# Two-layer encoder trunk: FFN's first weights split in the mixer's dead tiles, eps squares on other queues, a bank of its own for one edge product, weights in order of use

## Chip, cores and metric

The kernel runs on one core of a Trainium2 chip. The metric is the device time of one execution in microseconds; a kernel's time is the median of several executions. Between two kernels, a difference of some 0.2% is about what such a measurement can tell from none.

## What is computed

The trunk has two layers. Each is a mixer with RMS norms before and after it and a residual, then a squared-ReLU MLP (FFN) with the same frame. The two requests have 512 and 256 tokens, and the width is 1024. Cut to what matters here:

```python
for i in range(DEPTH):
    h = rms_norm(x, norm_mix_pre[i])
    mix = even_mixer(h, ...) if i % 2 == 0 else odd_mixer(h, ...)
    x = x + rms_norm(mix, norm_mix_post[i])
    h = rms_norm(x, norm_ffn_pre[i])
    f = jnp.square(jax.nn.relu(h @ ffn_w1[i])) @ ffn_w2[i]      # 1024 -> 4096 -> 1024
    x = x + rms_norm(f, norm_ffn_post[i])
```

## The kernel before, in words

All tiles hold features on the 128 partitions and tokens along the free dimension, 768 tokens in all (the 512 of the first request, the 256 of the second). A product in full precision is made of three matmuls per 128-row step: weights and activations are each split into a high and a low part (`hi` by a copy on ScalarE, `lo` by a subtraction on VectorE), and the three products hi*hi, lo*hi and hi*lo accumulate in one PSUM bank. The accumulators `acc` of the residual stay in SBUF.

**Order of work.** A scheduler with priorities lays out one program in order per engine; within an engine nothing overtakes. `tick`, `defer` and `settle` of `Trunk` put small finishing steps some number of matmul groups later than the step that they follow. `weave` mixes a list of fill steps into a list of main steps at a given rate.

**From mixer to FFN.** The mixer ends with `quarter`s of its output projection. The last one finishes the residual in three blocks of 256 tokens: `PostNorm` squares (`sq`, L451), sums the squares over partitions on TensorE (L272), makes `rstd` (L281 to L286), and writes the new `acc` (L481, L485) and the normalised `h` (L360, L361). FFN's class `Strassen` then multiplies by the first weight matrix in 32 units of 128 columns. The first four units go block by block (`units_a`), with weights split by `Strassen.first` (L540, L541) into tiles of the FFN's own pool, called `ht`. While four more units run, `blocks` builds the sums of activation blocks that a Strassen scheme (7 products instead of 8 on 2x2 blocks) needs (L573 to L580, tiles `tb`, `tt`, `ht`). From there `pair` computes two units at a time from weight sums `sw` (L606 to L610). The first and the last such pair (u = 3 and u = 15) are edge pairs: `X`, a PSUM tile, takes a first product "11", ScalarE copies it away (`p1`, written as `sg`, L660), and then a second product "12" by "21" is added into the same tile before it is put away (`put`).

**FFN's second matrix.** Class `Strassen2` (the functions `weights`, `add`, `keep`, `prep`) runs over pairs of hidden groups; j = 0 to 3 counts the output quarters within a pair. `weights` splits the sums and the raw weights (L794, L795) in the order s1 and s2 (`s12`), "12" and "22" (`raw`), s3 and s4 (`s34`), "11"; L854 adds a product from PSUM to `acc`. After the Strassen groups come plain quarters 4 to 7. With the group (2,3) runs a fill, `eps_sums`: it reloads the layer's input (`ex`), squares it on ScalarE (L404), adds the eight squares on GpSimd (L406) and sums them over partitions on TensorE (L414). Only the following post-norm needs the result.

**Odd mixer's start.** `sums` makes a block's `rstd` as a row (`rb`), and `by_token` turns `rb` into a column per token with TensorE (L426) and copies it on VectorE (L428).

Of the kernel before, what the change touches and what calls it, by code (L numbers as in the profile page):

```python
# [45 lines left out]
class Trunk:  # L46
# [292 lines left out]
class PreNorm:  # L339
# [55 lines left out]
    def eps_sums(self, xD, part):  # L395
# [12 lines left out]
        yield  # L408
        yield
        for s in range(2):  # L410
            ps = T.tps()
            n = SEQN[s] // CH
            for j in range(n):
                nc.tensor.matmul(ps[:, j:j + 1], lhsT=tot[s][:, j * CH:(j + 1) * CH], rhs=T.ones[:, 0:1], start=True,  # L414
                                 stop=True)
            v = T.cp.tile([128, 8], F32, tag="rsq_a", name="rsq_a", bufs=2)[:, 0:n]
            nc.vector.tensor_scalar(out=v, in0=ps[:, 0:n], scalar1=1.0 / 1024, scalar2=EPS, op0=ALU.mult, op1=ALU.add)
            nc.vector.scalar_tensor_tensor(out=self.rc[s][:, 0:n], in0=v, scalar=1024 * EPS, in1=v, op0=ALU.mult, op1=ALU.mult)
        yield

    def by_token(self, b):
        s, c0, n = b
        T, nc = self.T, self.T.nc
        ps = T.tps()
        for j in range(n // CH):
            nc.tensor.matmul(ps[:, j:j + 1], lhsT=self.rb[s][:, c0 + j * CH:c0 + (j + 1) * CH], rhs=T.ident[:, 0:1],  # L426
                             start=True, stop=True)
        nc.vector.tensor_copy(self.rc[s][:, c0 // CH:(c0 + n) // CH], ps[:, 0:n // CH])  # L428
        self.done.add(b)

# [89 lines left out]


class Strassen:

# [119 lines left out]
    def pair(self, u, edge):  # L643
# [19 lines left out]
        X = T.dps()[:, 0:HF]  # L663
        self.product(w["11"], "11", X, True, False)
        p1 = copy(X)
# [22 lines left out]
        else:  # L688
# [27 lines left out]
class StrassenK:  # L716
# [58 lines left out]

    def weights(self, j, first):

# [12 lines left out]
        def parts(n):  # L790
            return [T.wp.tile([128, 1024], F32R, tag=t, name=t, bufs=4)[:, 0:n] for t in ("whi", "wlo")]

        def split(x, hi, lo):
            nc.scalar.activation(out=hi, in_=x, func=AF.Copy)  # L794
# [8 lines left out]
        tt = (nc.vector if first else nc.gpsimd).tensor_tensor  # L803
        tt(out=s1, in0=a21, in1=a22, op=ALU.add)
# [4 lines left out]
        pl = parts(1024)  # L809
        split(raw[1], *pl)  # L810
        for m, name in enumerate(("12", "22")):
            w[name] = [t.rearrange("p (k m c) -> p m k c", k=4, m=2)[:, m] for t in pl]
# [28 lines left out]
    def group(self, gs, last):  # L841
# [5 lines left out]
        for j in range(4):  # L847
            w = self.weights(j, j == 0)
            u2 = self.u2[j]

            def add(ps, m, half):
                with hp():
                    for a, c in self.blocks(2 * j + m, half):
                        nc.vector.tensor_tensor(out=a, in0=a, in1=ps[:, c], op=ALU.add)  # L854

# [62 lines left out]

def ffn(T, layer, pre, xsrc, nxt, xdst):
    tc, nc = T.tc, T.nc  # L920
    with tc.tile_pool(name=f"ffn{layer}", bufs=1) as pool:
        hidD = tc.dram_tile([8, 4, 128, NT], F32, name=f"hidD{layer}")
        S = Strassen(T, pool, pre, pre.xs, layer, hidD)

        def evac(s, o, c0, n, m):
            gt = T.g0 if n == 512 else T.g1
            r = gt("fr")
            with tc.high_priority():
                nc.scalar.activation(out=r, in_=o, func=AF.Relu)
                nc.scalar.activation(out=r, in_=r, func=AF.Square)  # L930
            nc.sync.dma_start(out=hidD[m // 4, m % 4][:, SEQ0[s] + c0:SEQ0[s] + c0 + n], in_=r)

        srcs = [S.src[m] for m in range(NSTD)]
        evacs = [partial(evac, m=m) for m in range(NSTD)]
        run(T.units_a(S.first(4), pre, evacs))
        T.settle()
        fill = S.blocks()
        for m in range(4, NSTD):
            weave(T.unit_a(srcs[m], pre.h, evacs[m], True), fill, 0.5)
        run(fill)  # L940
# [6 lines left out]
        for i, g in enumerate(GROUPS):  # L947
# [12 lines left out]
            if not end and isinstance(GROUPS[i + 1], tuple):  # L960
                fill = K.prep(GROUPS[i + 1])
            elif g == EQ:
                fill, per = pre.eps_sums(xsrc, K.part), 0.4
            weave(steps, fill, per)
# [597 lines left out]
def even_layer(T):  # L1562
    tc, nc, I = T.tc, T.nc, T.I
    with tc.tile_pool(name="p0", bufs=7) as pool:
# [75 lines left out]
        run(T.quarter(I["evO"][3], mix_load(T, E.mixD, 3, place=place), acc, False, pn))  # L1640
    return pn.pre
PPB = 4
# [236 lines left out]
def odd_layer(T, pre):  # L1879
    tc, nc, I = T.tc, T.nc, T.I  # L1880
    with tc.tile_pool(name="p1", bufs=7) as pool:
# [37 lines left out]
    return pn.pre  # L1919


def trunk(tc, I, y):
    with ExitStack() as ctx:
        T = Trunk(ctx, tc, I, y)
        T.setup()
        pre = even_layer(T)
        pre = ffn(T, 0, pre, T.xa, (0, 1), T.xb)
        pre = odd_layer(T, pre)
        ffn(T, 1, pre, T.xc, None, y)

# [92 lines left out]
```

## Time and profile before

| | us |
|---|---|
| median of 3 runs (2297.16 to 2301.91) | 2301.15 |
| the profiled execution's own time | 2302.54 |
| its span (first to last instruction) | 2300.8 |
| TensorE busy | 2204.1 (96%) |
| VectorE busy | 1672.8 (73%) |
| ScalarE busy | 1061.9 (46%) |
| GpSimd busy | 667.9 (29%) |

The span is what the profiler records between first and last instruction; the time lies 1.7 us above it. TensorE is the engine to read by: what it is not busy is 96.7 us, and beside that there are stretches where its clock is granted at half.

### The profile page before, as it was taken

The numbers are of one execution on the slowest core, as the hardware profiler recorded it, in microseconds if no ns is written. First come the engines' busy times: TensorE is split into PE (matmuls) and PEld (weight loads), VectorE is DVE, ScalarE is ACT, GpSimd is POOL, SyncE is SP. The second block draws the span as 40 slices with busy tenths as digits, with TensorE's granted clock in tenths as the row PEclk, the third lists the DMA queues.
The fourth block names the chain that finished last, engine by engine and source line by source line (L and its number), as shares of the span: only waits on it lengthen the run. The fifth ranks groups of instructions, "written<-read, shape, count | busy, mean of one in ns | idle before, by whom it ended". The sixth has DMA issues, their size and how long they took to land.

```text
span 2300.8 us, 39195 instructions
## 1 busy us (share of the span) xinstructions
PE 2204.1 (96%) x14360; PEld 2038.9 (89%) x14360; DVE 1672.8 (73%) x3491; ACT 1061.9 (46%) x2140; POOL 667.9 (29%) x666
## 2 busy tenths in 40 slices
PE   8999999999998999999899899999998999999897
PEld 7888888998888999999889888988888999999887
DVE  8969858756556866678567758788766866688566
ACT  6655454334334544444324415555644644454332
POOL 2335133311104244220704330111004244320714
PEclk9999999999999999999999999999999999999999
DMA  4445235446343333544344245444533344544342
GB/s 148 125 130 159 84 117 158 140 142 189 119 129 117 114 120 128 185 142 151 104 151 127 98 145 161 153 156 143 175 111 124 100 135 129 162 165 138 116 129 92
DMA packets 188896, 311.23 MB, mean 135 GB/s; under 512 B 18912, under 2 KB 119328, under 8 KB 188704
## 3 DMA queue, kind: packets, MB, share of 16 engines
q1 hardware_dynamic: 188704, 308.73, 42.5%
q8 instruction: 113, 1.85, 0.3%
q14 instruction: 79, 0.65, 0.1%
HBM read 234.64 MB, written 74.02 MB: 134 GB/s over the span
## 4 chain that ended last, share of the span: by engine, by line
PE 70%; DVE 18%; issue 4%; ACT 3%; DMA 3%; POOL 2%; SPq 0%; POOLq 0%; ACTq 0%; DVEq 0%
PE dps L208 6%; PE dps L209 6%; PE dps L210 6%; PE dps L154 4%; PE dps L152 4%; PE dps L153 4%; PE dps L187 3%; PE dps L627 3%; PE dps L628 3%; PE dps L629 3%; PE dps L189 3%; PE dps L188 3%; DVE acc L481 2%; PE mps L629 2%; PE mps L627 2%
## 5 line engine op out<-in xcount | busy, mean ns | idle before, releaser
L208 PE MATMUL dps<-mh,whi 128*128 128x256 f32 (+1 forms) x800 | 270.5, 338 | 1.2 <-DVE acc L219 1.1
L209 PE MATMUL dps<-mh,whi 128*128 128x256 f32 (+1 forms) x800 | 265.5, 332 | 0.0
L210 PE MATMUL dps<-mh,wlo 128*128 128x256 f32 (+1 forms) x800 | 264.8, 331 | 0.0
L187 PE MATMUL dps<-whi,h 128*128 128x256 f32 x864 | 260.4, 301 | 1.9 <-ACT gv L1695 1.5
L152 PE MATMUL dps<-h,whi 128*128 128x256 f32 (+1 forms) x728 | 251.7, 346 | 0.0
L189 PE MATMUL dps<-whi,h 128*128 128x256 f32 x864 | 245.7, 284 | 2.2 <-DVE h L361 2.2
L188 PE MATMUL dps<-wlo,h 128*128 128x256 f32 x864 | 245.4, 284 | 0.0
L154 PE MATMUL dps<-h,wlo 128*128 128x256 f32 (+1 forms) x728 | 243.1, 334 | 0.0
L153 PE MATMUL dps<-h,whi 128*128 128x256 f32 (+1 forms) x728 | 242.8, 334 | 0.0
L119 ACT ACTIVATE whi<-raw 128x1024 fp32r<-128x1024 f32 x140 | 147.7, 1057 | 162.6 <-PE dps L209 59.0
L120 DVE TENSOR_TENSOR wlo<-raw,whi 128x1024 fp32r<-128x1024 f32 x140 | 177.5, 1271 | 48.4 <-ACT whi L119 47.2
L187 PEld LDWEIGHTS dps<-whi,h 128*128 128x128 f32 x864 | 166.0, 192 | 13.7 <-issue 9.0
L188 PEld LDWEIGHTS dps<-wlo,h 128*128 128x128 f32 x864 | 166.4, 193 | 3.3 <-issue 2.2
L189 PEld LDWEIGHTS dps<-whi,h 128*128 128x128 f32 x864 | 166.0, 192 | 2.8 <-DVE h L361 2.8
L208 PEld LDWEIGHTS dps<-mh,whi 128*128 128x128 f32 x800 | 152.5, 191 | 17.4 <-DVE acc L219 2.6
L219 DVE TENSOR_TENSOR acc<-acc,dps 128x512 f32<-128x512 f32 (+1 forms) x208 | 100.7, 486 | 91.0 <-PE dps L210 90.9
L210 PEld LDWEIGHTS dps<-mh,wlo 128*128 128x128 f32 x800 | 152.1, 190 | 14.8
L455 POOL TENSOR_TENSOR sq<-sq 128x256 f32<-128x256 f32 x79 | 64.6, 818 | 345.0 <-ACT sq L451 344.6
L209 PEld LDWEIGHTS dps<-mh,whi 128*128 128x128 f32 x800 | 152.5, 191 | 13.5
L152 PEld LDWEIGHTS dps<-h,whi 128*128 128x128 f32 x728 | 138.6, 190 | 17.0 <-issue 4.9
L153 PEld LDWEIGHTS dps<-h,whi 128*128 128x128 f32 x728 | 138.8, 191 | 13.7 <-issue 1.7
L154 PEld LDWEIGHTS dps<-h,wlo 128*128 128x128 f32 x728 | 138.6, 190 | 13.5
(377 smaller groups left out, 6391.8 us busy)
## 6 DMA issues: line engine op xcount, KB each, us to landing
raw<-in_f SPq DMA_DIRECT2D x128, 512.0 KB, 3.9
hidD<-hc SPq DMA_DIRECT2D x104, 192.0 KB, 1.9
xt<-hidD SPq DMA_DIRECT2D x40, 384.0 KB, 3.8
rr<-acsD SPq DMA_DIRECT2D x48, 256.0 KB, 3.7
raw<-in_evB SPq DMA_DIRECT2D x24, 512.0 KB, 3.7
rl<-retD SPq DMA_DIRECT2D x48, 256.0 KB, 2.8
raw<-hidD SPq DMA_DIRECT2D x24, 512.0 KB, 3.8
stk<-qkD SPq DMA_DIRECT2D x96, 128.0 KB, 2.8
```

The lines of the kernel that those rows point to most:

```text
L119: nc.scalar.activation(out=hi, in_=raw, func=AF.Copy)
L120: nc.vector.tensor_tensor(out=lo, in0=raw, in1=hi, op=ALU.subtract)
L152: nc.tensor.matmul(o, lhsT=hi[:, k, :], rhs=hh[k][:, sl], start=k == 0, stop=False)
L153: nc.tensor.matmul(o, lhsT=hi[:, k, :], rhs=hl[k][:, sl], start=False, stop=False)
L154: nc.tensor.matmul(o, lhsT=lo[:, k, :], rhs=hh[k][:, sl], start=False, stop=k == NKT - 1)
L187: nc.tensor.matmul(o, lhsT=hh[k][:, sl], rhs=hi[:, k % 4, :], start=k == 0, stop=False)
L188: nc.tensor.matmul(o, lhsT=hh[k][:, sl], rhs=lo[:, k % 4, :], start=False, stop=False)
L189: nc.tensor.matmul(o, lhsT=hl[k][:, sl], rhs=hi[:, k % 4, :], start=False, stop=k == NKT - 1)
L208: nc.tensor.matmul(o, lhsT=hi[:, k, ms], rhs=hh[k][:, sl], start=k == 0, stop=False)
L209: nc.tensor.matmul(o, lhsT=hi[:, k, ms], rhs=hl[k][:, sl], start=False, stop=False)
L210: nc.tensor.matmul(o, lhsT=lo[:, k, ms], rhs=hh[k][:, sl], start=False, stop=k == 3)
L627: nc.tensor.matmul(o, lhsT=hi[:, k, :], rhs=hh[k], start=first and k == 0, stop=False, **f)
```

## The change

- `ffn_first` runs the first four units inside the mixer's pool, before it closes. Their weights are split in halves of 512 columns (L555 and L556 after) into 16 tiles called `fw`, which take the places of mixer tiles that nothing reads any more (`xtok`, `cr0`, `bc0`, `hb` in the even layer; `st0`, `ang`, `v` in the odd).
- `eps_sums` squares in place in one 128x768 tile per step, its adds go from GpSimd to VectorE, and `issue_after` puts both behind the last split and the last add of the Strassen groups on their own queues (order only, no semaphore).
- In an edge pair the product "12" by "21" gets a PSUM tile of its own, `V`, and VectorE adds `V` and `p1` into an SBUF tile (`c11`), four times in the kernel.
- For j = 3 `weights` splits in the order "11", `raw`, `s34`, `s12`.
- A block counts as done when its `rb` is written, `defer` keeps its list sorted, and the odd layer's `by_token` is deferred by 3 steps instead of 6.

```diff
     def defer(self, n, f):
         self.late.append([n, f])
+        self.late.sort(key=lambda i: i[0])
...
-        while b not in self.done:
+        while b not in self.done and self.T.late:
             self.T.late.pop(0)[1]()
...
-        T.defer(FT2, partial(self.by_token, b))
+        self.done.add(b)
+        T.defer(FT2 if self.first else FT3, partial(self.by_token, b))
...
-        tot = [T.g0("et"), T.g1("et")]
+        tot = part("et")
         for k in range(NKT):
-            x = part("ex")
+            x = part("ex") if k else tot
             nc.sync.dma_start(out=x, in_=xD[k])
-            for s in range(2):
-                xs = x[:, SEQ0[s]:SEQ0[s] + SEQN[s]]
-                nc.scalar.activation(out=xs if k else tot[s], in_=xs, func=AF.Square)
+            with ExitStack() as ctx:
+                for i in tail:
+                    ctx.enter_context(T.tc.issue_after(i.ins))
+                nc.scalar.activation(out=x, in_=x, func=AF.Square)
                 if k:
-                    nc.gpsimd.tensor_tensor(out=tot[s], in0=tot[s], in1=xs, op=ALU.add)
+                    nc.vector.tensor_tensor(out=tot, in0=tot, in1=x, op=ALU.add)
...
-    def first(self, n):
+    def first(self, tiles):
...
-        for i in range(n):
+        for i in range(4):
             raw = T.wp.tile([128, 1024], F32, tag="raw", name="raw", bufs=3)
             nc.sync.dma_start(out=raw, in_=self.src[i])
-            hi, lo = (self.slot()[:, 0:1024] for _ in range(2))
-            nc.scalar.activation(out=hi, in_=raw, func=AF.Copy)
-            nc.vector.tensor_tensor(out=lo, in0=raw, in1=hi, op=ALU.subtract)
-            ws.append([t.rearrange("p (a b) -> p a b", b=128) for t in (hi, lo)])
+            hi, lo = ([tiles() for _ in range(2)] for _ in range(2))
+            for j in range(2):
+                x = raw[:, 512 * j:512 * j + 512]
+                nc.scalar.activation(out=hi[j], in_=x, func=AF.Copy)
+                nc.vector.tensor_tensor(out=lo[j], in0=x, in1=hi[j], op=ALU.subtract)
+            ws.append((Halves(hi), Halves(lo)))
...
-            self.product(w["12"], "21", X, False, True)
-            self.put(m0, 0, X, act=True)
+            V = T.dps()[:, 0:HF]
+            self.product(w["12"], "21", V, True, True)
+            c11 = g()
+            add(c11, V, p1)
+            self.put(m0, 0, c11, act=True)
...
-            split_sums(s12, ("s1", "s2"))
+        if last:
+            split_11()
+            split_raw()
+        else:
+            split_sums(s12, ("s1", "s2"))
         tt(out=s3, in0=a11, in1=a21, op=ALU.subtract)
         tt(out=s4, in0=a12, in1=s2, op=ALU.subtract)
...
-        split_sums(s34, ("s3", "s4"))
-        w["11"] = [t.rearrange("p (k c) -> p k c", k=4) for t in parts(512)]
-        split(a11, *w["11"])
+        if last:
+            split_sums(s34, ("s3", "s4"))
+            split_sums(s12, ("s1", "s2"))
+        else:
+            split_raw()
+            split_sums(s34, ("s3", "s4"))
+            split_11()
```

**VectorE where the Strassen blocks begin (even layer).** Before, the four sums `sw` of the first edge pair wait for a DMA alone and stand ahead of the block sums `tt`:

```order
L600 TENSOR_TENSOR wlo<-raw,whi 128x1024 [waits DMAHW6_49,Activation_49]
L606 TENSOR_TENSOR sw<-raw 128x512 [waits DMAHW4_49]
L609 TENSOR_TENSOR sw<-raw 128x512
L607 TENSOR_TENSOR sw<-sw,raw 128x512 [waits DVE_49]
L610 TENSOR_TENSOR sw<-raw,sw 128x512 [waits DVE_49]
L600 TENSOR_TENSOR wlo<-sw,whi 128x1024 [waits Activation_49]
L574 SCALAR_TENSOR_TENSOR tt<-acc_6826,negw,tb 128x128 [waits Activation_49]
```

After the change the first of them waits for TensorE too (the tile `sw` lies where an `fw` tile lay; what it waits for is the last matmul of the first four units), and the block sums `tt` begin among them:

```order
L615 TENSOR_TENSOR wlo<-raw,whi 128x1024 [waits Activation_49]
L621 TENSOR_TENSOR sw<-raw 128x512 [waits DMAHW4_49,PE_49]
L624 TENSOR_TENSOR sw<-raw 128x512
L622 TENSOR_TENSOR sw<-sw,raw 128x512 [waits DVE_49]
L589 SCALAR_TENSOR_TENSOR tt<-acc_6826,negw,tb 128x128 [waits Activation_49]
L625 TENSOR_TENSOR sw<-raw,sw 128x512 [waits DVE_49]
L590 SCALAR_TENSOR_TENSOR tt<-acc_6830,pv,tt 128x128 [waits DVE_49]
L591 SCALAR_TENSOR_TENSOR tt<-acc_6830,pv,tb 128x128
L615 TENSOR_TENSOR wlo<-sw,whi 128x1024 [waits Activation_49]
```

So four sums and one split that stood clear of the blocks now stand in them, behind a wait for TensorE.

**ScalarE in the groups after the eps squares.** Before, the squares L404 stand between the splits and copies that the second Strassen group (2,3) begins with:

```order
L404 ACTIVATE ex<-ex 128x512
L769 ACTIVATE b_12576<-xt 128x768
L404 ACTIVATE ex<-ex 128x256
L769 ACTIVATE b_12582<-xt 128x768
L794 ACTIVATE whi<-raw 128x512
L404 ACTIVATE ex<-ex 128x512
```

After, the copies (now L788) and the splits (now L813) follow on one another, and the squares (now L408) stand between the splits (L121) of the plain quarters 4 and 5:

```order
L788 ACTIVATE b_12598<-xt 128x768
L788 ACTIVATE b_12604<-xt 128x768
L813 ACTIVATE whi<-raw 128x512
...
L408 ACTIVATE ex<-ex 128x768 x4
L121 ACTIVATE whi<-raw 128x1024 x2
...
L121 ACTIVATE whi<-raw 128x1024
L408 ACTIVATE ex<-ex 128x768
L121 ACTIVATE whi<-raw 128x1024
L408 ACTIVATE ex<-ex 128x768 x2
```

**TensorE at the odd mixer's start.** Before, the transposes `tps<-ident` of two blocks come together, behind the partition sums (L272) of the third block:

```order
L153 MATMUL dps<-h,whi 128x512
L154 MATMUL dps<-h,wlo 128x512
L272 MATMUL tps<-psq,ones 128x256
L426 MATMUL tps<-ident,rb_13511 128x1 x4
L152 MATMUL dps<-h,whi 128x256
```

After, those of the first block stand alone, 18 matmuls of 256 columns behind that block's own partition sums (L274), and ahead of the second block's:

```order
L190 MATMUL dps<-wlo,h 128x256
L191 MATMUL dps<-whi,h 128x256
L430 MATMUL tps<-ident,rb_13516 128x1 x2
L189 MATMUL dps<-whi,h 128x256
L190 MATMUL dps<-wlo,h 128x256
```

The first block's two moved ahead by 44 rows of TensorE's queue, while ScalarE's order around `rstd` is as before.

## Rows read from the trace of the kernel before

**Rows 1.** The page's first part: busy us, share of the span, instructions of each engine.

```profile
PE 2204.1 (96%) x14360; PEld 2038.9 (89%) x14360; DVE 1672.8 (73%) x3491; ACT 1061.9 (46%) x2140; POOL 667.9 (29%) x666
```

**Rows 2.** Waits of TensorE: waiting line, releaser, us in total, times, longest.

```profile
PE mps L832 <- DVE acc L854: 13.0, 2, 6.6
PE dps L152 <- ACT ht L540: 11.7, 2, 5.9
...
PE dps L627 <- ACT sg L660: 5.1, 4, 1.6
...
PE tps L426 <- DVE rc L428: 2.4, 1, 2.4
...
PE dps L834 <- DVE wlo L795: 2.6, 2, 1.3
...
PE dps L832 <- ACT whi L794: 2.2, 4, 0.5
```

**Rows 3.** Windows: busy us and count per engine, granted clock PEclk, DMA share, GB/s.

```profile
727.50:734.00 6.50, 6.05 (x33) 6.05 (x34) 4.86 (x9) 2.70 (x6) 0.00 (x0) 0.59 0.78 250
1111.70:1121.90 10.20, 6.20 (x19) 6.20 (x20) 6.40 (x10) 2.61 (x5) 6.35 (x5) 0.50 0.18 58
1159.50:1162.90 3.40, 3.40 (x13) 3.40 (x12) 2.38 (x6) 2.45 (x6) 0.00 (x0) 0.50 0.59 219
1299.40:1302.80 3.40, 3.40 (x18) 3.40 (x18) 2.98 (x17) 0.00 (x0) 0.00 (x0) 0.50 0.02 7
```

**Rows 4.** Timeline of ScalarE, 690 to 730 us: start, duration; in brackets idle before, releaser.

```profile
697.30 0.42 ACT L451 ACTIVATE sq<-acc 128x256 f32<-128x256 f32 x1 [1.01 <-DVE acc L219]
...
725.60 1.04 ACT L540 ACTIVATE ht<-raw 128x1024 fp32r<-128x1024 f32 x1
...
728.74 0.49 ACT L360 ACTIVATE h<-acc,pv 128x256 fp32r<-128x256 f32 x1
```

**Rows 5.** Timeline of GpSimd from 1095 us.

```profile
1101.58 16.56 POOL L406 TENSOR_TENSOR et<-et,ex 128x512 f32<-128x512 f32 x14
```

**Rows 6.** Timeline of ScalarE from 1098 us.

```profile
1106.79 0.94 ACT L404 ACTIVATE ex<-ex 128x512 f32<-128x512 f32 x2 [4.05 <-POOL et L406]
...
1109.21 0.83 ACT L769 ACTIVATE b<-xt 128x768 fp32r<-128x768 f32 x1
```

**Rows 7.** Timeline of VectorE from 1098 us.

```profile
1110.07 1.50 DVE L770 TENSOR_TENSOR b<-xt,b 128x768 fp32r<-128x768 f32 x1 [7.70 <-ACT b L769]
```

**Rows 8.** Windows over plain quarter 4 and over the Strassen blocks, columns as in rows 3.

```profile
1184.00:1208.00 24.00, 24.00 (x141) 21.24 (x140) 11.04 (x23) 3.19 (x3) 0.00 (x0) 1.00 0.37 121
766.00:791.00 25.00, 23.42 (x136) 21.30 (x135) 24.22 (x50) 16.97 (x37) 5.57 (x4) 1.00 0.21 72
```

**Rows 9.** Timeline of TensorE in the first edge pair.

```profile
787.90 0.45 PE L627 MATMUL dps<-h,whi 128*128 128x384 f32 x1 [1.58 <-ACT sg L660]
```

**Rows 10.** Timeline of VectorE, 757 to 793 us.

```profile
760.72 0.69 DVE L606 TENSOR_TENSOR sw<-raw 128x512 f32<-128x512 f32 x1 [1.36 <-DMA raw<-in_f]
...
763.74 1.23 DVE L600 TENSOR_TENSOR wlo<-sw,whi 128x1024 fp32r<-128x1024 f32 x1 [0.40 <-ACT whi L599]
...
770.26 1.51 DVE L574 SCALAR_TENSOR_TENSOR tt<-acc,negw,tb 128x256 f32<-128x256 f32 x1
...
789.20 1.46 DVE L580 TENSOR_TENSOR ht<-tt,ht 128x512 fp32r<-128x512 f32 x2
```

**Rows 11.** Timeline of GpSimd from 757 us.

```profile
770.02 1.48 POOL L607 TENSOR_TENSOR sw<-sw,raw 128x512 f32<-128x512 f32 x1
```

**Rows 12.** Timeline of TensorE at the odd mixer's start.

```profile
1283.04 0.59 PE L272 MATMUL tps<-psq,ones 128*128 128x256 f32 x2
...
1286.53 0.39 PE L187 MATMUL dps<-whi,h 128*128 128x256 f32 x1 [1.47 <-ACT gv L1695]
```

**Rows 13.** Timeline of ScalarE there.

```profile
1288.54 0.47 ACT L281 ACTIVATE rstd<-tps,eps 128x256 f32<-128x256 f32 x1
```

**Rows 14.** Timeline of VectorE there.

```profile
1291.09 0.43 DVE L286 SCALAR_TENSOR_TENSOR rb<-rstd 128x256 f32<-128x256 f32 x1
```

More of the change, by code (lines that the diff above doesn't have):

```diff
@@ L34 @@
 FT2 = 6
+FT3 = 3
 EL = 2
@@ L413, in eps_sums @@
             for j in range(n):
-                nc.tensor.matmul(ps[:, j:j + 1], lhsT=tot[s][:, j * CH:(j + 1) * CH], rhs=T.ones[:, 0:1], start=True,
-                                 stop=True)
+                c = SEQ0[s] + j * CH
+                nc.tensor.matmul(ps[:, j:j + 1], lhsT=tot[:, c:c + CH], rhs=T.ones[:, 0:1], start=True, stop=True)
             v = T.cp.tile([128, 8], F32, tag="rsq_a", name="rsq_a", bufs=2)[:, 0:n]
@@ L428, in by_token @@
         nc.vector.tensor_copy(self.rc[s][:, c0 // CH:(c0 + n) // CH], ps[:, 0:n // CH])
-        self.done.add(b)
 class PostNorm:
@@ L519, with __init__, __getitem__ @@
 WP0 = 900
+class Halves:
+    def __init__(self, tiles):
+        self.t = [t.rearrange("p (k c) -> p k c", k=4) for t in tiles]
+    def __getitem__(self, i):
+        return self.t[i[1] // 4][:, i[1] % 4, i[2]]
 class Strassen:
@@ L663, in pair @@
         X = T.dps()[:, 0:HF]
-        self.product(w["11"], "11", X, True, False)
+        self.product(w["11"], "11", X, True, edge)
         p1 = copy(X)
@@ L722, in __init__ @@
         self.u2 = None
+        self.tail = [None, None]
     def part(self, name="xt"):
@@ L774, in prep_last, with weights @@
         T.tc.cur_priority = p
-    def weights(self, j, first):
+    def weights(self, j, first, last):
         T, nc = self.T, self.nc
@@ L793, in split @@
         def split(x, hi, lo):
-            nc.scalar.activation(out=hi, in_=x, func=AF.Copy)
+            self.tail[1] = nc.scalar.activation(out=hi, in_=x, func=AF.Copy)
             nc.vector.tensor_tensor(out=lo, in0=x, in1=hi, op=ALU.subtract)
@@ L803, in weights, with split_raw, split_11 @@
         tt = (nc.vector if first else nc.gpsimd).tensor_tensor
+        def split_raw():
+            pl = parts(1024)
+            split(raw[1], *pl)
+            for m, name in enumerate(("12", "22")):
+                w[name] = [t.rearrange("p (k m c) -> p m k c", k=4, m=2)[:, m] for t in pl]
+        def split_11():
+            w["11"] = [t.rearrange("p (k c) -> p k c", k=4) for t in parts(512)]
+            split(a11, *w["11"])
         tt(out=s1, in0=a21, in1=a22, op=ALU.add)
         tt(out=s2, in0=s1, in1=a11, op=ALU.subtract)
-        split_sums(s12, ("s1", "s2"))
+        if last:
[3 more added lines that the diff above has]
+            split_sums(s12, ("s1", "s2"))
         tt(out=s3, in0=a11, in1=a21, op=ALU.subtract)
         tt(out=s4, in0=a12, in1=s2, op=ALU.subtract)
[L809 to L812, printed above, removed]
-        split_sums(s34, ("s3", "s4"))
-        w["11"] = [t.rearrange("p (k c) -> p k c", k=4) for t in parts(512)]
-        split(a11, *w["11"])
+        if last:
[5 more added lines that the diff above has]
+            split_11()
         T.tc.cur_priority = p
@@ L847, in group @@
         for j in range(4):
-            w = self.weights(j, j == 0)
+            w = self.weights(j, j == 0, j == 3)
             u2 = self.u2[j]
@@ L853, in add @@
                     for a, c in self.blocks(2 * j + m, half):
-                        nc.vector.tensor_tensor(out=a, in0=a, in1=ps[:, c], op=ALU.add)
+                        self.tail[0] = nc.vector.tensor_tensor(out=a, in0=a, in1=ps[:, c], op=ALU.add)
             def keep(ps, copy):
@@ L916, with ffn_first, evac, ffn @@
 PR = 0.28
-def ffn(T, layer, pre, xsrc, nxt, xdst):
+def ffn_first(T, layer, pre, tiles):
     tc, nc = T.tc, T.nc
-    with tc.tile_pool(name=f"ffn{layer}", bufs=1) as pool:
[L922 to L936, printed above, removed]
+    hidD = tc.dram_tile([8, 4, 128, NT], F32, name=f"hidD{layer}")
+    S = Strassen(T, None, pre, pre.xs, layer, hidD)
+    def evac(s, o, c0, n, m):
+        gt = T.g0 if n == 512 else T.g1
+        r = gt("fr")
+        with tc.high_priority():
+            nc.scalar.activation(out=r, in_=o, func=AF.Relu)
+            nc.scalar.activation(out=r, in_=r, func=AF.Square)
+        nc.sync.dma_start(out=hidD[m // 4, m % 4][:, SEQ0[s] + c0:SEQ0[s] + c0 + n], in_=r)
+    S.evacs = [partial(evac, m=m) for m in range(NSTD)]
+    run(T.units_a(S.first(tiles), pre, S.evacs))
+    T.settle()
+    return S
+def ffn(T, layer, S, xsrc, nxt, xdst):
+    tc, nc, pre, hidD = T.tc, T.nc, S.pre, S.hidD
+    with tc.tile_pool(name=f"ffn{layer}", bufs=1) as pool:
+        S.pool = pool
         fill = S.blocks()
         for m in range(4, NSTD):
-            weave(T.unit_a(srcs[m], pre.h, evacs[m], True), fill, 0.5)
+            weave(T.unit_a(S.src[m], pre.h, S.evacs[m], True), fill, 0.5)
         run(fill)
@@ L962, in ffn @@
             elif g == EQ:
-                fill, per = pre.eps_sums(xsrc, K.part), 0.4
+                fill, per = pre.eps_sums(xsrc, K.part, K.tail), 0.4
             weave(steps, fill, per)
@@ L1633, in even_layer, with tiles @@
         pn = PostNorm(T, acc, (1, 0), I["xT"], (2, 0), T.xa)
+        free = iter([("xtok", 512, 7)] * 7 + [("cr0", 516, 3)] * 3 + [("bc0", 512, 3)] * 2 + [("hb", 512, 4)] * 4)
+        def tiles():
+            tag, n, bufs = next(free)
+            return pool.tile([128, n], F32R, tag=tag, name="fw", bufs=bufs)[:, 0:512]
         t = by_seq([[pool.tile([128, NT], F32R, tag="mh", name="mh", bufs=4) for _ in range(4)], []])
@@ L1640, in even_layer @@
         run(T.quarter(I["evO"][3], mix_load(T, E.mixD, 3, place=place), acc, False, pn))
-    return pn.pre
+        return ffn_first(T, 0, pn.pre, tiles)
 PPB = 4
@@ L1913, in odd_layer, with tiles @@
         pn = PostNorm(T, acc, (1, 1), T.xb, (2, 1), T.xc)
+        free = iter([("st0", 6)] * 6 + [("ang00", 1), ("ang10", 1)] + [("v", 8)] * 8)
+        def tiles():
+            tag, bufs = next(free)
+            return pool.tile([128, 512], F32R, tag=tag, name="fw", bufs=bufs)
         t = by_seq([[pool.tile([128, NT], F32R, tag="mh", name="mo", bufs=5) for _ in range(n)] for n in (4, 1)])
@@ L1918, in odd_layer @@
         run(T.quarter(I["odO"][2], mix_load(T, O.mixD, 2, place=place), acc, False, pn))
-    return pn.pre
+        return ffn_first(T, 1, pn.pre, tiles)
 def trunk(tc, I, y):
@@ L1925, in trunk @@
         T.setup()
[L1926 to L1929, printed above, removed]
+        S = even_layer(T)
+        pre = ffn(T, 0, S, T.xa, (0, 1), T.xb)
+        S = odd_layer(T, pre)
+        ffn(T, 1, S, T.xc, None, y)
 def cols_a(w):
```

2 lines of the change are left out of this document (1 added, 1 removed).

## The prediction, made before the changed kernel ran

> **What bounds the kernel now.** I read three views, in this order. The page's first part: TensorE is busy for 96% of the span, every other engine for less than three quarters [rows 1]. So an edit counts only where it shortens a wait of TensorE or gives it back its clock. Then TensorE's waits by releaser [rows 2]: six entries belong to the places that the diff touches, 37.0 us together. Last the windows behind these waits [rows 3]: there the granted clock is 0.50, or an average near it, which is the lower of its two levels, 1.2 GHz. A wait so costs twice: its own length, and half of the time that TensorE then works at half clock.
>
> **First weights.** L152 waits 11.7 us in two waits, one per layer, for ScalarE's split L540 [rows 2]. The split runs at 725.60 [rows 4], late because its `ht` tile lies in a pool that opens only when the mixer's closes. With `fw` in dead tiles of the mixer the splits stand ahead of the post-norm's squares `sq` in ScalarE's queue. The clock: over 727.50 to 734.00 it averages 0.59, so 0.41 of 6.5 us, 2.7 us, are lost, less half of the 0.45 us in which TensorE stood anyway: 2.4 us [rows 3]. Twice that, with the 11.7: **16.5 us**. What is late next is `h` of the second block, whose last piece ends at 729.2 [rows 4]. TensorE would start at 720.7 (the split's end, 726.6, less the longest wait, 5.9 [rows 2, 4]) and has the first block's 96 matmuls before it, 10.4 us by 33 in 6.05 us at a mean clock of 0.59 [rows 3]: 731.1, a cover of 1.9 us, and ScalarE and VectorE, rid of the splits there, come earlier. ScalarE pays 8 half splits, about 0.5 us each by the 1.04 us of a whole one [rows 4], among the squares; these have 1.01 us of idle time ahead of each, ten times in a row [rows 4], so 4.2 us of splits hide there. Without that cover they would make `h` late by as much.
>
> **eps squares.** L832 waits 13.0 us in two waits for L854 [rows 2]. The chain behind it: GpSimd's 14 adds take 16.56 us [rows 5], ScalarE's squares wait for them (4.05 us at 1106.79) and so the copy `b` (L769) starts at 1109.21 [rows 6]; VectorE waits 7.70 us for that copy [rows 7], and L854 stands behind. The change takes squares and adds out of all three queues there. The clock behind the wait: 6.20 us of work at 0.50 [rows 3], 3.1 us per layer. Together 13.0 + 6.2 = **19.2 us**. The moved work: eight squares of 0.83 us (a copy of the same shape, L769 [rows 6]), 6.6 us, and seven adds of at most 1.50 us (L770, the same shape [rows 7]), 10.5 us. It lands in plain quarter 4, where in 24 us VectorE is busy for 11.04, ScalarE for 3.19 and GpSimd not at all [rows 8]: 13 and 21 us are free. I cost it at nothing. If the cover fails, the adds `acc` that free TensorE's banks stand behind an add that waits for a square; this is a rival below.
>
> **j = 3 weights.** L834 waits 2.6 us for the subtraction L795, L832 2.2 us for the copy L794, of which a small part lies elsewhere [rows 2]. In the new order the "11" split comes first, and it is wanted first. The second group's waits are followed by 3.40 us of work at half clock [rows 3], 1.7 us, per layer. 4.8 + 3.4 = **8.2 us**.
>
> **Edge pairs.** L627 waits 5.1 us in four waits for the copy L660 [rows 2], because the second product goes into the bank that is being copied. The first pair's is 1.58 us [rows 9], in each layer; the last pairs' are the rest, 5.1 - 3.2 = **1.9 us**, and they go. VectorE pays an add of 384 columns per pair, under 0.8 us (half of L770's 1.50 [rows 7]); only the put waits for it.
>
> In the first pair the wait goes too, but what is late next stands there already. The next product takes `ht` of the last block sum, which ends at 789.20 + 1.46 = 790.66 [rows 10]. TensorE restarts at 787.90 [rows 9] and comes to it 21 matmuls later, 3.4 us by 19 matmuls in 6.20 us at half clock [rows 3], at 791.3: 0.6 us to spare. Without the wait of 1.58 it is 1.0 us short. And the change adds to VectorE's queue ahead of it. The sums `sw` now wait for TensorE's last matmul of the first units (they lie on `fw` tiles); before, they ran at 760.72, after 1.36 us of idle time [rows 10]. Four of 0.69 and a split of 1.23 [rows 10], 4.0 us, move into a stretch where VectorE is busy for 24.22 of 25 us [rows 8]: less 0.78 idle, 3.2 us later. Behind the waiting `sw` stand the block sums `tt`, and behind these TensorE. The new wait is 1.0 + 3.2 = 4.2 us. Does the clock fall behind it? 2.4 us [rows 2], with 1.47 us shortly before [rows 12], is followed by 3.4 us at 0.50 [rows 3]; 1.58 us is not followed by any, the mean stays 1.00 [rows 8]. 4.2 is nearer to the former, so I add 1.7. Per layer -1.58 + 4.2 + 1.7 = 4.3, in both layers **8.6 us lost**. Bounds: if the sums fit between others after all, 1.0 - 1.58, a gain of 0.6 per layer. From above: beside GpSimd's sum of 1.48 us [rows 11] a VectorE operation on 256 columns took 1.51 us [rows 10]; four sums of 1.51 in place of 0.69 make the wait 7.5 and the loss 7.6 per layer.
>
> The Trainium skill has a rule for this (SBUF — State Buffer, section Who interferes with whom): a VectorE instruction with two SBUF inputs and a GpSimd instruction that reads SBUF use one shared port, and whichever starts second waits for the whole of the other. By this rule each of the four sums may meet one GpSimd sum; the pair of rows above agrees with it for one meeting. Taken in full it would make the wait 7.5 us, against the 4.2 of the sum; GpSimd is busy in that stretch for only 5.57 of 25 us, so most sums should not meet one.
>
> **Odd layer's by_token.** Before, L426 waits 2.4 us once [rows 2]. Now the first block's transposes stand 18 matmuls behind its partition sums of 1283.04; with the wait of 1.47 us that ended at 1286.53 TensorE comes to them at about 1286.9 [rows 12]. ScalarE's `rstd` starts only at 1288.54, behind splits in its queue [rows 13], and `rb` ends at 1291.09 + 0.43 [rows 14]: 4.6 us of waiting. For the next two blocks I estimate 1 us each: from L281's start to the end of `rb` the first took 3.0 us [rows 13, 14], and 18 matmuls, 2.2 to 3.5 us at full clock, stand between. 6.6 - 2.4 = **4.2 us lost**; the half-clock stretch that is there stays. Bounds: 2.2 (no wait for the later blocks) and 8.9 (2.5 us each and a second half-clock stretch).
>
> **Sum.** 16.5 + 19.2 + 8.2 + 1.9 = 45.8 gained, 8.6 + 4.2 = 12.8 given back, 33.0 net. From the profiled execution's 2302.54 this gives 2269.5; the median of the runs lies 1.4 lower, so 2268.
>
> **Rivals.**
> - *The new waits stay small*: the sums fit into VectorE's gaps and by_token waits at its lower bound. 8.6 becomes a gain of 1.2, 4.2 becomes 2.2: 2256. For it: work that TensorE gates slips together with it. Against: 24.22 of 25 us [rows 8].
> - *The new waits are at their upper bounds*: 15.2 and 8.9 lost, 2279.
> - *The eps work blocks where it goes*: an add `et` waits for a square behind a split that waits for a weight slot, and `acc` adds wait behind it. The wait of 13.0 + 6.2 us moves instead of going: 2278 with half of it, 2287 with all.
> - *The clock does not come back*: other short waits keep it low at the six places. 4.8 + 6.2 + 3.4 = 14.4 less: 2282. Against: 0.50 stands only behind the waits.
> - *Nothing is regained*: the post-norm, not the weights, sets the restart, and the next waits take the rest: 2301. Against: the releaser in rows 2 is L540.
> - *Slower*: the `fw` splits stand ahead of `sq` in ScalarE's queue and wait for their loads, with the whole post-norm behind them. From about 10 us on (ten gaps of 1.01 [rows 4]) each us delays TensorE in each layer. To be 0.2% slower than before (4.6 us, about what a measurement here tells from no change), 38 us must go, 19 per layer, so the loads must be 29 us late. 2306 or more. Against: a square `sq` waits for VectorE in every row there, so ScalarE is early.
>
> **How the numbers follow.** Forecast with its terms 0.42 (its own range 2261 to 2275), small new waits 0.20, large ones 0.13, eps work blocks 0.10, clock stays low 0.06, nothing regained 0.04, slower 0.05. The range 2252 to 2284 takes in the bounds of the two unknown waits and the clock's case, and leaves out the last two and a part of the eps case, some 0.15 with the edges. Faster by over 0.2%: 0.91, within: 0.04, slower: 0.05.
>
> **What will show it.** Right: no wait of L152 or its successor for a split of the first weights; no wait of Strassen2's first "22" product behind `acc`; clock 1.00 in both places; new waits for `ht` in the first edge pair and for `rb` in the odd layer. Wrong: TensorE waiting in plain quarters 4 and 5, half-clock stretches without a wait, or a first-unit wait for `h`.

## The result and the profile after

The changed kernel takes 2276.44 us (median of 4 runs, 2275.11 to 2277.80), against 2301.53 us before (4 runs): 0.9898 of the time, 95% interval 0.988 to 0.9917, so 25.1 us less. The time lies in the predicted range and on the predicted side; of the 33 us forecast, 8 did not come. The text ahead has three slips about the kernel: `blocks` runs with two more units and not four, the class of the Strassen groups is called `StrassenK`, and the plain quarters behind the second group are 4 and 5 (`GROUPS`).

The first part of the page of the changed kernel:

```profile
PE 2197.5 (97%) x14360; PEld 2029.4 (89%) x14360; DVE 1674.0 (74%) x3517; ACT 1059.2 (47%) x2132; POOL 630.1 (28%) x638
```

TensorE is busy for 6.6 us less than before, with the same matmuls, since less of its work ran at half clock (the mean granted clock of the profiled execution is 0.989, before 0.983); the rest of the gain is waiting. Waits of TensorE in the changed kernel (line, releaser, us in total, times, longest), which answer to [rows 2]:

```profile
PE dps L210 <- DVE acc L221: 5.4, 8, 0.9
PE dps L642 <- ACT ht L594: 5.1, 2, 2.6
PE tps L430 <- DVE rb L288: 4.6, 2, 4.1
...
PE mps L868 <- DVE wlo L814: 2.0, 2, 1.1
PE dps L642 <- ACT sg L675: 1.9, 2, 1.0
...
PE dps L643 <- DVE ht L595: 0.9, 2, 0.6
```

The 13.0 and 11.7 us of [rows 2] are gone. The wait for `rc` has become waits for `rb`. The two entries for the block sums `ht` are new, the entries for `wlo` and for `sg` are smaller, and the one for `acc` (L210) is larger: 5.4 us in eight waits, before 4.0 us in six. Four windows, columns as in [rows 3]: the first units, the start of the second Strassen group, the first edge pair, the odd mixer's start.

```profile
719.00:727.00 8.00, 8.00 (x70) 8.00 (x69) 8.00 (x16) 4.42 (x11) 4.79 (x6) 1.00 0.42 123
1103.20:1109.60 6.40, 6.40 (x39) 6.40 (x38) 4.02 (x6) 2.24 (x3) 1.45 (x2) 1.00 0.02 4
781.20:788.00 6.80, 6.23 (x20) 6.07 (x20) 3.65 (x5) 2.55 (x4) 1.01 (x1) 0.50 0.34 106
1274.80:1279.60 4.80, 4.73 (x20) 4.58 (x21) 3.21 (x13) 1.14 (x2) 0.00 (x0) 0.50 0.60 218
```

At the first two places, where [rows 3] has 0.59 and 0.50, the granted clock is 1.00. In the last two windows it is 0.50: the stretch in the first edge pair is new, the one in the odd mixer is longer than the 3.4 us of before.

Since both kernels issue the same 14360 matmuls in nearly the same order, the start of the n-th in both traces shows where the lead is won and lost. The changed kernel less the one before, us, worked out from such starts:

| stage | even layer | odd layer |
|---|---|---|
| mixer up to its last quarter | -2.2 | - |
| first units | -9.7 | -8.7 |
| first edge pair | +5.0 | +4.9 |
| from there to the first Strassen group's j = 3 | +2.2 | +1.3 |
| first group's j = 3 | -0.4 | -0.7 |
| between the groups | -0.8 | 0.0 |
| second group's start | -9.5 | -9.6 |
| second group's j = 3 | -2.1 | -1.9 |
| plain quarters 4 and 5 | +0.9 | +0.4 |
| odd mixer's start (`by_token`) | | +4.2 |
| rest of the odd mixer, its last quarters | | +2.1 |

The sum is -24.7; the spans differ by 24.8. The first stage is hardly touched by the change. Over the kernels below its length varies from -3.1 to +2.3 us against before, with where the half-clock stretches fall, so a difference of 2 or 3 us between two totals is read from the stages.

### The profile page after: what moved, and what is told of

It reads as the page before. It is cut to its first block, busy times and chain, and to the rows that moved or that the text cites. A ratio compares the mean times of both kernels' runs of the same rounds, so it can differ in the third digit from the quotient of the medians.

```text
span 2276.0 us, 39172 instructions
## 1 busy us (share of the span) xinstructions
PE 2197.5 (97%) x14360; PEld 2029.4 (89%) x14360; DVE 1674.0 (74%) x3517; ACT 1059.2 (47%) x2132; POOL 630.1 (28%) x638
## 4 chain that ended last, share of the span: by engine, by line
PE 62%; DVE 21%; DMA 7%; issue 4%; ACT 4%; POOL 2%; SPq 0%; DVEq 0%; POOLq 0%; ACTq 0%
PE dps L210 4%; PE dps L154 4%; PE dps L156 4%; PE dps L155 4%; PE dps L211 4%; PE dps L212 4%; PE dps L189 3%; PE dps L190 3%; PE dps L191 3%; PE dps L642 3%; PE dps L643 3%; PE dps L644 3%; DVE wlo L122 2%; PE mps L644 2%; PE mps L642 2%
## 5 line engine op out<-in xcount | busy, mean ns | idle before, releaser
L210 PE MATMUL dps<-mh,whi 128*128 128x256 f32 (+1 forms) x800 | 271.5, 339 | 2.6 <-DVE acc L221 1.5
L121 ACT ACTIVATE whi<-raw 128x1024 fp32r<-128x1024 f32 x140 | 147.5, 1055 | 125.7 <-PE dps L155 50.1
L210 PEld LDWEIGHTS dps<-mh,whi 128*128 128x128 f32 x800 | 152.5, 191 | 21.1 <-ACT acc L218 3.4
```

Source lines behind the costliest of these rows:

```text
L210: nc.tensor.matmul(o, lhsT=hi[:, k, ms], rhs=hh[k][:, sl], start=k == 0, stop=False)
```

## The experiments

All edits are to the changed kernel. Times are medians; each is set against runs of the kernel before that were made beside it on the same chip. No run separates the new bank of the last edge pairs, or the sorting in `defer`.

| run | us | less than before | ratio, 95% interval |
|---|---|---|---|
| the change | 2276.44 | 25.1 | 0.9898 [0.9880, 0.9917] |
| 1 first pair's sums on GpSimd | 2282.57 | 17.9 | 0.9923 [0.9907, 0.9938] |
| 2 first pair's own bank undone | 2278.55 | 21.9 | 0.9908 [0.9891, 0.9925] |
| 3 transposes deferred by 9 | 2269.08 | 31.3 | 0.9864 [0.9847, 0.9881] |
| 4 old order for j = 3 | 2277.99 | 22.4 | 0.9896 [0.9881, 0.9911] |
| 5 second pair's sums late | 2269.35 | 32.9 | 0.9859 [0.9844, 0.9874] |
| 6 runs 3 and 5 together | 2259.73 | 42.5 | 0.9819 [0.9806, 0.9832] |
| 7 eps squares undone | 2293.93 | 8.3 | 0.9975 [0.9962, 0.9988] |
| 8 first weights undone | 2284.68 | 17.5 | 0.9931 [0.9918, 0.9944] |
| 9 run 6, first pair's bank undone | 2257.47 | 45.0 | 0.9809 [0.9790, 0.9829] |
| 10 run 6, eps adds on GpSimd | 2266.39 | 36.1 | 0.9845 [0.9826, 0.9865] |

**The first edge pair: runs 1, 5, 8.** What the changed kernel's trace shows there, on TensorE, VectorE and GpSimd in turn:

```profile
780.92 0.44 PE L642 MATMUL dps<-ht,whi 128*128 128x384 f32 x1 [2.55 <-ACT ht L594]
781.93 0.69 PE L643 MATMUL dps<-ht,whi 128*128 128x384 f32 x1 [0.57 <-DVE ht L595]
```

```profile
753.54 0.69 DVE L621 TENSOR_TENSOR sw<-raw 128x512 f32<-128x512 f32 x1 [5.71 <-PE dps L156]
...
756.75 1.22 DVE L615 TENSOR_TENSOR wlo<-sw,whi 128x1024 fp32r<-128x1024 f32 x1
...
760.25 1.38 DVE L589 SCALAR_TENSOR_TENSOR tt<-acc,negw,tb 128x128 f32<-128x128 f32 x1
761.55 1.51 DVE L592 SCALAR_TENSOR_TENSOR tt<-acc,pv,tt 128x256 f32<-128x256 f32 x1
762.98 1.38 DVE L590 SCALAR_TENSOR_TENSOR tt<-acc,pv,tt 128x128 f32<-128x128 f32 x1
764.28 2.38 DVE L595 TENSOR_TENSOR ht<-tt,ht 128x512 fp32r<-128x512 f32 x2
...
780.74 0.54 DVE L670 TENSOR_TENSOR sg<-sg,dps 128x384 f32<-128x384 f32 x1
781.20 0.68 DVE L595 TENSOR_TENSOR ht<-tt,ht 128x512 fp32r<-128x512 f32 x1
```

```profile
759.97 1.50 POOL L621 TENSOR_TENSOR sw<-raw 128x512 f32<-128x512 f32 x1 [20.83 <-DMA raw<-in_f]
761.44 1.34 POOL L624 TENSOR_TENSOR sw<-raw 128x512 f32<-128x512 f32 x1
```

TensorE waits 2.55 + 0.57 us for `ht`. VectorE stands idle for 5.71 us before the first `sw`. It ends the last block sum at 781.88, 8.8 us earlier than before (790.66 [rows 10]), but TensorE is 11.9 us ahead when it comes to the pair: against TensorE the last sum is 3.1 us later. Beside the moved sums there is something else to see: from 760 to 766.6, while GpSimd makes four sums for the second pair, a step `tt` takes 1.38 or 1.51 us where the same shapes take 0.34 and 0.48 elsewhere in the stretch.

Run 1 takes the four sums from VectorE:

```diff
-        tt = (nc.vector if first else nc.gpsimd).tensor_tensor
+        tt = nc.gpsimd.tensor_tensor
```

> The changed kernel, but the four sums of the first edge pair are made by GpSimd and not by VectorE, in both layers. Queue theory: the first pair waits for its last block sum because four sums (2.8 us) stand behind a wait for TensorE in VectorE's queue, ahead of the block sums; without them the wait of 3.1 us shrinks to about 0.5 and the half-clock stretch behind it goes, (2.6 + 3.4) x 2 = 12 us, so about 2264. Rival, contention: GpSimd's four sums of 1.3 to 1.5 us each hold up VectorE's block sums by as much as they took from its queue; the wait stays at 3 us or more, 2276 or above.

The time went up. On VectorE and on GpSimd:

```profile
756.59 1.38 DVE L591 SCALAR_TENSOR_TENSOR tt<-acc,pv,tb 128x128 f32<-128x128 f32 x1
...
759.29 1.34 DVE L592 SCALAR_TENSOR_TENSOR tt<-acc,pv,tt 128x128 f32<-128x128 f32 x1
...
765.51 3.48 DVE L595 TENSOR_TENSOR ht<-tt,ht 128x512 fp32r<-128x512 f32 x2
```

```profile
755.21 1.30 POOL L621 TENSOR_TENSOR sw<-raw 128x512 f32<-128x512 f32 x1 [14.48 <-PE dps L156]
```

Nearly every step beside a GpSimd sum now takes as long as the sum, and the two `ht` subtractions take 3.48 us. The first pair loses 6.4 and 6.6 us against before, more than the 5.0 and 4.9 of the change. Moving the sums to an idle engine took nothing off VectorE here: the rival, contention, held.

Run 5 takes GpSimd's sums for the second pair away from the block sums instead (`mark` is a column that only orders GpSimd's work):

```diff
+                if k == 3 and t0:
+                    self.mark = nc.gpsimd.tensor_tensor(out=T.mark, in0=t4[:, 0:1], in1=t4[:, 0:1], op=ALU.add)
...
+            if u == NSTD // 2 + 1:
+                ctx.enter_context(T.tc.issue_after(self.mark.ins))
             w = self.weights(u, u == NSTD // 2)
```

> The changed kernel; GpSimd first reads one column of the last block sum (an add of 128x1), and only then makes the four sums of the second pair (u = 4), so these stand behind VectorE's block sums and not beside them, in both layers. Contention theory: beside GpSimd's four sums four of VectorE's steps took 1.38, 1.51, 1.38 and 2.38 us where the same steps take 0.34, 0.47, 0.34 and 1.28 alone, 4.2 us; without them the last block sum is ready before TensorE asks, the wait of 3.1 us and the half-clock stretch behind it (3.4) go in both layers, 13 us: about 2263. Rival, queue order: the wait comes only from the sums that VectorE itself makes, GpSimd is a bystander: 2274 to 2278.

On VectorE and on GpSimd of this run, and the wait that is left on TensorE:

```profile
761.67 0.35 DVE L590 SCALAR_TENSOR_TENSOR tt<-acc,negw,tb 128x128 f32<-128x128 f32 x1
761.93 0.48 DVE L593 SCALAR_TENSOR_TENSOR tt<-acc,pv,tt 128x256 f32<-128x256 f32 x1
762.33 0.35 DVE L591 SCALAR_TENSOR_TENSOR tt<-acc,pv,tt 128x128 f32<-128x128 f32 x1
762.59 1.29 DVE L596 TENSOR_TENSOR ht<-tt,ht 128x512 fp32r<-128x512 f32 x2
...
778.41 1.48 DVE L596 TENSOR_TENSOR ht<-tt,ht 128x512 fp32r<-128x512 f32 x1
```

```profile
777.51 0.57 POOL L598 TENSOR_TENSOR mark<-tt 128x1 f32<-128x1 f32 x1 [36.94 <-DVE tt L593]
778.04 1.29 POOL L624 TENSOR_TENSOR sw<-raw 128x512 f32<-128x512 f32 x1
```

```profile
PE dps L646 <- DVE ht L596: 0.7, 2, 0.3
```

The steps are back at 0.35 and 0.48, the two subtractions at 1.29 (2.38 in the changed kernel). Only the last subtraction still meets a GpSimd sum, and of the first pair's wait 0.3 us per layer is left. No half-clock stretch stands behind it, and the stage is at -1.2 in both layers: some 6.2 us per layer less than with the change, 12.3 together. The profiled executions (2277.80 and 2267.02) differ by 10.8 us, the medians by 7.1, or 7.8 as differences to the kernel before; the four executions of run 5 lie between 2265.25 and 2272.25, and the stages elsewhere differ by 1 or 2 us where this edit does nothing.

Run 8 goes back to weights split in the FFN's pool (`first` as in the diff's minus lines, its four units run after the pool opens).

> The changed kernel with the first weights split in the FFN's own pool again, after the mixer's pool has closed. Theory: 9.2 and 8.3 us come back at the first product, but the sums of the first pair no longer wait for TensorE, and the new wait for the block sums with its half clock, 3.6 + 3.4 us per layer, goes; of 17.5 us some 10 to 14 are given back: 2280 to 2284. Rival: the late block sums have another cause (the bank V, or GpSimd alone) and stay: about 2294.

```profile
PE dps L154 <- ACT ht L553: 11.8, 2, 5.9
```

The old wait is back at its old size (11.7 in [rows 2]), the first units give back their 18 us, and the first pair is at -0.7 and -0.6. So with either removed, the sums that now stand in VectorE's queue (run 8) or GpSimd's sums beside the block sums (run 5), at most 0.8 us of waiting for `ht` is left in a pair. But only the first is new. Before the change GpSimd's sums stood beside the block sums too:

```profile
767.58 2.76 DVE L580 TENSOR_TENSOR ht<-tt,ht 128x256 fp32r<-128x256 f32 x2
770.26 1.51 DVE L574 SCALAR_TENSOR_TENSOR tt<-acc,negw,tb 128x256 f32<-128x256 f32 x1
771.70 1.51 DVE L576 SCALAR_TENSOR_TENSOR tt<-acc,pv,tb 128x256 f32<-128x256 f32 x1
```

Against the same shapes elsewhere in the stretch (0.41 and 0.47) this is 4.0 us more. The changed kernel's slow steps come to 4.2 us more, and those of run 8 to 4.2. So the moved sums are what the change adds, and run 5 makes up for them by taking away a hold-up that the kernel before had already.

**The own bank: runs 2 and 9.** Both let the first pair's second product go into the copied bank again:

```diff
-        self.product(w["11"], "11", X, True, edge)
+        self.product(w["11"], "11", X, True, edge and u == 15)
...
-            V = T.dps()[:, 0:HF]
-            self.product(w["12"], "21", V, True, True)
-            c11 = g()
-            add(c11, V, p1)
+            if u == 15:
+                V = T.dps()[:, 0:HF]
+                self.product(w["12"], "21", V, True, True)
+                c11 = g()
+                add(c11, V, p1)
+            else:
+                self.product(w["12"], "21", X, False, True)
+                c11 = X
```

> The changed kernel, but in the first edge pair the second product goes into the copied bank X again, as before the change (the last pair keeps its own bank). Theory: the first pair is set by the late block sums, so the wait of about 1.6 us for the copy comes back and the wait for the block sums gets shorter by as much; VectorE even has an add of 0.5 us less ahead of the last one. Time 2275 to 2277. Rival (the step of the prediction): the bank of its own gives back 1.58 us per layer, so without it 2279 to 2280.

> The sixth run's kernel (GpSimd's sums late, transposes deferred by 9), but in the first edge pair the second product goes into the copied bank again. Theory: with the block sums in time the own bank is worth what the prediction said, a wait of some 1.6 us for the copy in each layer, 3.2 us: about 2263. Rival: the copy is made early enough by now (ScalarE is ahead of the block sums) and the bank is worth nothing: 2259 to 2260.

In run 2 TensorE waits once, for the copy, in place of the two waits for `ht`:

```profile
783.36 0.69 PE L642 MATMUL dps<-h,whi 128*128 128x384 f32 x1 [4.46 <-ACT sg L675]
```

The stage is at +5.7 and +5.1, 0.7 and 0.3 more than with the change. The wait for the copy is 4.46 us and not the 1.6 that was expected, since the copy stands behind the late block sums in ScalarE's queue. The time, 2278.55, lies between the two figures, and its interval overlaps that of the change: it decides nothing, the trace does. In run 9, where the block sums are in time, all waits for that copy are:

```profile
PE dps L645 <- ACT sg L680: 2.4, 4, 1.0
```

Two of these are 1.0 us each and lie elsewhere (below), so about 0.25 is left for each first pair, and the stage is at -1.2, within 0.1 of run 6. The rival held: with the block sums in time the copy is in time too, and the bank is worth nothing that the trace shows. That the copy was late in [rows 9] because ScalarE's queue was held up by the block sums fits this. Run 9 is the fastest kernel of the study, but not told apart from run 6.

**Transposes: run 3**, `FT3 = 3` to `FT3 = 9`.

> The changed kernel, with the odd layer's transposes deferred by 9 steps and not 3. Theory: what TensorE waits for there is only the place of the transposes in its queue; 54 matmuls behind the partition sums rb is ready, the three waits of 4.1, 0.7 and 0.4 us go, and with them the half-clock stretch that costs 2.4 us: 7 to 8 us less, about 2269. Rival: the norm chain behind the transposes is needed as soon, and the wait moves to its consumers: 2274 to 2277.

```profile
1266.00:1272.00 6.00, 5.95 (x46) 5.60 (x45) 2.79 (x2) 4.67 (x10) 4.93 (x6) 1.00 0.20 61
1272.00:1284.00 12.00, 12.00 (x70) 10.57 (x69) 10.45 (x33) 6.97 (x14) 0.00 (x0) 1.00 0.61 211
```

From 1266 to 1284 TensorE is busy throughout and its clock is 1.00; no wait of L430 is left. The stage is at about -4 to -5 us against before, by where it is cut, 8 to 9 us better than with the change; the time is 6 to 7 us better. The theory held: the place in the queue was all.

**Weights of j = 3: run 4** (`self.weights(j, j == 0, False)`).

> The changed kernel, with the weights of j = 3 split in the old order. Theory: the new order saves what the two traces show, 0.7 us in the first group and 0.7 + 0.4 + 1.7 (clock) in the second, per layer, 3.0 to 3.5: about 2283. Rival: it only moves a wait from the first product to the product with s2, and saves nothing: 2276.

```profile
PE dps L866 <- ACT whi L813: 2.2, 4, 0.5
...
PE dps L868 <- DVE wlo L814: 1.8, 2, 1.3
```

The waits of the old order are there with 4.0 us in place of 4.8, yet the second group's stage is at -2.4 and +0.1 against before, the new order's at -2.1 and -1.9. The first group's is 0.0 in both layers, the new order's -0.4 and -0.7. By the stages the order alone is so worth 2.7 us, much nearer to the rival's nothing than to the theory's 6 to 7; the two times, with intervals 0.9880 to 0.9917 and 0.9881 to 0.9911, are not told apart. In the even layer's second group the old order is even 0.3 better, and brings no half-clock stretch with it; most of the 2.7 lies in the odd layer's second group, where the old order still has such a stretch of 3.4 us (2172.5 to 2175.9 in run 4).

**eps squares: run 7** (the function as it was, with GpSimd's adds).

> The changed kernel with the eps squares as before the change: adds on GpSimd, beside the start of the second Strassen group, nothing behind the last split. Theory: both traces agree on 9.9 and 8.8 us between the places before and after this wait, so 19 us come back, and the late second group brings back some of the waits for the j = 3 weights, which the old order alone did not: 2296 to 2300. Rival: the eps squares cost only their own wait of 6.5 us per layer, the half clock behind it has another cause: about 2289.

```profile
PE mps L865 <- DVE acc L887: 14.1, 3, 6.8
```

The wait is back, and 17 us of the medians, which lies between the two figures; by the stage of the second group's start it is 8.5 and 8.9. j = 3 is at -1.1 and -1.6 in place of -2.1 and -1.9, 1.3 us: a part of what I had put down to the order hangs on the eps squares. Together this is 18.7 us, as the theory had it.

**Runs 6 and 10.**

> The edit of the run before together with transposes deferred by 9 steps (third run). The two places lie in different stages, so the gains add: 13 and 7 us, about 2256. If the first edit brings nothing, 2269.

The gains of runs 3 and 5 are both there: 42.5 us less than before, where the two differences to the change would give 39.1.

> The sixth run's kernel, but the eps adds behind the paired quarters are made by GpSimd, which is idle there, and not by VectorE. Theory: a wait of 0.7 to 0.9 us at the start of plain quarter 5's steps, where the adds of the accumulators stand behind an eps add that waits for its square, goes, in one layer or both: 2258 to 2259, in the trace no wait for an accumulator in that stretch. Rival: GpSimd's adds hold up VectorE's splits with their two SBUF inputs and TensorE waits for these: 2262 or more.

On TensorE, VectorE and GpSimd of run 10:

```profile
1151.13 0.69 PE L871 MATMUL dps<-ht,whi 128*128 128x384 f32 x1 [2.43 <-DVE acc L893]
```

```profile
1144.32 5.76 DVE L1602 TENSOR_TENSOR mh<-raw,mh 128x512 fp32r<-128x512 f32 x3
```

```profile
1143.10 13.34 POOL L411 TENSOR_TENSOR et<-et,ex 128x768 f32<-128x768 f32 x6 [4.46 <-ACT ex L409]
```

Three subtractions, the first of 512 columns and two of 256, took 5.76 us (the same three took 1.35 in the changed kernel) beside GpSimd's adds; an add of `acc` stood behind them and TensorE behind that, 2.43 us, with a half-clock stretch. The second group's j = 3, where this falls, is worse than in run 6 by 4.3 and 4.5 us. The rival held, as in run 1.

## Why the prediction was right or wrong

- **First weights, 16.5 us: right**, 18.4 in the stage. Half of the 1.9 more is a wait that went too and was left out of the sum, that for VectorE's half of the same split:

```profile
PE dps L154 <- DVE ht L541: 0.9, 2, 0.5
```

  Not in the sum either: in the odd layer's last quarter an `acc` add stands behind the new subtractions, 1.2 us, which run 8 does not have (0.0).
- **eps squares, 19.2 us: right**, 19.1 in the stages, 17 by run 7. "I cost it at nothing" was wrong by up to 1.2 us in this trace, the named rival at small size; in runs 1, 2, 4 and 6, with the same eps work, the even layer's quarter 4 is as long as before. VectorE of the changed kernel in plain quarter 4:

```profile
1177.35 0.96 DVE L410 TENSOR_TENSOR et<-et,ex 128x768 f32<-128x768 f32 x1 [1.73 <-ACT ex L408]
1178.22 0.41 DVE L221 TENSOR_TENSOR acc<-acc,dps 128x256 f32<-128x256 f32 x1
```

  The add `et` waits 1.73 us for its square, `acc` stands behind it, and TensorE waits 0.56 us for that.
- **j = 3, 8.2 us: wrong**, the term was mis-sized. The traces show 5.0 in its stages, and run 4 that the order is worth about 2.7 of it. I had taken the waits [rows 2] to go without a new one behind them. In the new order the split of `s34`, wanted by the second product, is late in its turn (L868, 2.0 us in two waits), and TensorE waits another 0.8 us for `u` (L866). And I had put the waits and the half clock [rows 3] down to the order alone, while a part of them hung on the eps squares just before (runs 4 and 7); that changes whose gain it is, not the sum.
- **Last edge pairs, 1.9 us: wrong.** The step "the last pairs' are the rest" failed. Two of the four waits of L627 lie in an ordinary pair (u = 14), which the change doesn't touch; the same wait is there afterwards:

```profile
943.75 0.44 PE L642 MATMUL dps<-h,whi 128*128 128x384 f32 x1 [0.96 <-ACT sg L675]
```

- **First edge pair, 8.6 us lost: right in kind**, 9.9 lost, and the number is near by luck, since two misses partly cancel: the wait is 3.1 in place of 4.2, the half-clock stretch 6.8 us in place of 3.4. The cause was VectorE's queue, as reckoned: the last block sum is 3.1 us later against TensorE, where the sum had 3.2, and run 8, without the moved sums, loses nothing. The upper bound did not come about: the moved sums took 0.69 us each and met no GpSimd sum. What the prediction lacked is that GpSimd's sums for the second pair had held up the block sums all along, by some 4 us, and that moving these would more than pay for the loss (run 5). The rule of the Trainium skill (SBUF — State Buffer, section Who interferes with whom) points at this: by it a VectorE instruction with two inputs in SBUF and a GpSimd instruction that reads SBUF exclude one another for the whole of an instruction. Steps of 1.38 beside sums of 1.34 (run 1), and 0.35 without (run 5), agree with it. That "`sw` lies on `fw` tiles" is not shown: the trace has only the wait of the first `sw` for that matmul, and the closing of the mixer's pool, whose place the pool of `sw` takes, would make the same wait.
- **The 1.58 us of the copy: cause wrong.** The bank of its own doesn't bring them; with the block sums in time the copied bank costs about 0.25 us (run 9).
- **by_token, 4.2 us lost: right in kind**, 4.2 in the stage, and the number is luck in part. ScalarE and VectorE of the changed kernel:

```profile
1271.77 0.47 ACT L283 ACTIVATE rstd<-tps,eps 128x256 f32<-128x256 f32 x1
```

```profile
1274.30 0.43 DVE L288 SCALAR_TENSOR_TENSOR rb<-rstd 128x256 f32<-128x256 f32 x1
```

  The wait for the first block is 4.1 us, those of the two others 0.7 and 0.4 in place of 1 each, the half-clock stretch 6.8 us in place of 3.4. So the waits are 1.4 us shorter than in the sum, and "the half-clock stretch that is there stays" was wrong by 1.7 us the other way.
- **Not foreseen:** 3.5 us of short waits between the first edge pair and the first Strassen group. Over runs 1 to 10 the same stages lie between -0.2 and +2.8 us with no edit there; what sets them is open.

## What to carry to other kernels

A list of waits by releaser gives places, not causes: before a wait is booked to an edit, find its instruction in the timeline, and what stood ahead of the releaser in its queue. Waits close to one another are not additive, since one late engine makes several. Work moved to an idle GpSimd was not free here: VectorE's steps beside it, with two tiles in SBUF to read, took longer (1.38 us in place of 0.34 in run 1, 5.76 in place of 1.35 in run 10). Moving GpSimd's work in time (run 5) did what moving work to GpSimd could not. And a hold-up found in the changed kernel is looked for in the kernel before as well, before the change is blamed for it.

## What the hardware showed

The same wait in the first edge pair, 2.6 + 0.6 us, is followed by half-clock stretches of different length: at the window that is at half clock in the changed kernel, run 3 is at full clock again some 3.4 us after its stretch began. Windows of the changed kernel and of run 3:

```profile
784.60:788.00 3.40, 3.40 (x12) 3.40 (x12) 0.99 (x2) 0.00 (x0) 1.01 (x1) 0.50 0.37 135
```

```profile
785.70:789.00 3.30, 3.30 (x12) 3.30 (x11) 1.78 (x2) 0.36 (x1) 0.00 (x0) 0.50 0.72 218
789.10:792.40 3.30, 3.30 (x21) 3.30 (x20) 1.73 (x3) 1.06 (x1) 2.82 (x3) 1.00 0.02 5
```

12 matmuls in 3.3 us against 21. The changed kernel's stretch began at 781.2, between the two waits, and lasted 6.8 us; run 3's began at 785.6, 1.4 us after the second wait, and lasted 3.4 us. The first pair's stages differ by 1.3 and 1.4 us for it, with no edit there. Such lengths, and not the edits, make some of the difference between two kernels with the same waits.
